# adaLN columns on VectorE alone from transposed weights, held order in the light expert steps, two output stores from ACT's queue

## The chip, the cores and the metric

The kernel runs on one core of a Trainium2 chip. The time is device microseconds of one execution, as the median of several runs. Engines are named as in the profile: PE (TensorE; PEld is its weight load), DVE (VectorE, V in the code), ACT (ScalarE, S), POOL (GpSimd, G), SP (SyncE, whose queue issues nearly all loads).

## The reference, cut to what matters

```
x: (1, 256, 1024); two layers
cond = silu(c)
for l in range(2):
    ada = cond @ w_ada[l] + b_ada[l]              # w_ada[l]: 1024 x 6144
    sh1, sc1, gt1, sh2, sc2, gt2 = split(ada, 6)
    h = rmsnorm(x, g_mix[l]) * (1 + sc1) + sh1
    z = h @ w_in[l]                               # q, k, v, forget, S5 input, two gates
    y_att = forgetting_attention(q, k, v, log_f) @ w_proj_att[l]
    y_ssm = s5(u, ...) @ w_proj_ssm[l]
    x = x + gt1 * ((g_att * y_att + g_ssm * y_ssm) @ w_out[l])
    h2 = rmsnorm(x, g_ffn[l]) * (1 + sc2) + sh2
    f = swiglu(h2, w1, w3, w2) if l == 0 else moe(h2)   # moe: top 2 of 8 experts
    x = x + gt2 * f
out = rmsnorm(x, g_final)
```

All is float32. D_FF is 2816, which the kernel cuts into 11 blocks of 256. The part in question is `ada`: 6144 columns for each layer, in 12 chunks of 512. The first four chunks of layer 0 are made at the very start by another function (`ada_first`); 20 chunks are left.

## The kernel before, in words

All 256 tokens are held on chip with the channels on partitions (`x_t`, 8 slices of 128). The weights are streamed from HBM in 1 MB loads, issued by SP in program order (`load_raw`, L211), before the MoE into a ring of three buffers `raw` (`RB = 3`). A load whose buffer is still read waits, and with it all loads behind it on SP's queue. For a product, `load_parts` splits each weight into a rounded part `wh` (ACT, L227) and a rest `wl` (DVE, L228, two instructions of 128x1024 for each load), with four buffers each, and PE takes three products for one (`dense_T`, L248).

The program has five stretches: layer 0's mixer (0 to 320 us), the dense FFN (to 495), layer 1's mixer (to 750), the MoE (to 1403, when its last load has landed) and the tail.

In the dense FFN, block j takes two loads of w13d (A and B here), 96 matmuls `mm` (L248), a gate on ACT and DVE (`fsg` L1000, `fgh` L268), and then one load of w2d (C here) and 48 matmuls `facc` (L988) for block j-1.

`ada_chunk(l, ch, E)` computes 512 adaLN columns. The tables `AT0`, `AT1` (keys are places in the mixers of layers 0 and 1) and `ATF` (block of the FFN, layer, chunk, engine) say when. With E = V it makes two loads of 1 MB through the `raw` ring, and one multiply (L324) and seven multiply-adds (L326) of 128x512 on DVE: the input channels lie on partitions, and a column of `cond` is the scalar. With E = G it makes four loads of 512 KB from POOL's queue into buffers of its own (L333), and multiplies and adds on POOL (L334, L338, L340). Either way the sum over the 128 partitions is left to `finish`, which the next chunk or `ada_flush` runs: four PE transposes (L347), four accumulating reads on ACT (L350) and an add of the bias on DVE (L351). 13 chunks are on V and 7 on G. POOL also builds the S5 tables, for layer 0 at the start and for layer 1 in the first FFN blocks.

In the MoE six lightly loaded experts run one after the other (`light`; n is 32 or 64 rows), and two heavy ones are put between their steps (`straight`). A step j of a light expert is `stage1(j)` (16 matmuls `s`, L1539, then the gate `sgS` on ACT L1544 and DVE L1545), in whose middle stands `turn_g` for block j-1 (transposes `gT`, L1527, copied to `gS` by ACT), and then `stage2(j-1)` (matmuls `y`, L1554). So stands the code; a scheduler orders the instructions of an engine, and `queued(E)` pins what is inside it behind the last instruction that engine E has been given so far. The loads go through a ring of 14 buffers of 1 MB.

`finish(ch)` (L1195 on) ends the program: the last norm, and four stores of 256 KB, all issued by SP (L1223).

Of the kernel before, what the change touches and what calls it, by code (L numbers as in the profile page):

```python
# [9 lines left out]
F32 = mybir.dt.float32  # L10
# [4 lines left out]
AF = mybir.ActivationFunctionType  # L15
# [12 lines left out]
FIRST_W = (1, 5)  # L28


AT0 = [('g1', 4, 'V'), ('g3', 5, 'V'), ('qk1', 8, 'V'), ('g2', 9, 'G'), ('p0', 6, 'V'), ('g0', 7, 'V'),
       ('o1', 10, 'V')]
AT1 = [('g0', 4, 'G'), ('g2', 5, 'V'), ('p1', 8, 'G'), ('g3', 9, 'G'), ('p0', 7, 'V'), ('o1', 10, 'V'),
       ('qk1', 11, 'G')]
ATF = [(8, 1, 6, 'G'), (6, 0, 11, 'V'), (4, 1, 2, 'G'), (7, 1, 3, 'V'), (9, 1, 0, 'V'), (1, 1, 1, 'V')]
P = 128
D = 1024
KC = 8
# [59 lines left out]


@with_exitstack  # L100
def trunk_kernel(ctx: ExitStack, tc: tile.TileContext, xT, sm, co, w_ada0, w_ada, w_in, w_v, s5bc, w_glu,
                 w_pa, w_ps, w_out, w13d, w2d, w13m, w2m, out, dbg=None, stop=None):
    nc = tc.nc
    V, S, G, PE = nc.vector, nc.scalar, nc.gpsimd, nc.tensor
# [23 lines left out]
    @contextmanager  # L128
    def queued(*engines):

        with ExitStack() as st:
            for E in engines:
                last = next((i for i in reversed(nc.cur_bb.bb.instructions) if i.engine == E.engine), None)
                if last is not None:
                    st.enter_context(tc.issue_after(last))
            yield
# [27 lines left out]
        return bank(("ms0", "ms0", "ms1", "ms1") if pair is None else (f"ms{pair}",), name)  # L164


    RB, AB, HB = 3, 2, 4
    QMAX = 2 * 520

    slots = {"raw": [(wp, "raw", RB)], "wh": [(wp, "wh", HB)], "wl": [(wp, "wl", HB)]}  # L170
# [32 lines left out]
    def load_raw(src, rows, cols):  # L203

        if ring:
            t = turn[0]
            turn[0] += 1
            return ring[t % len(ring)].rearrange("p (r c) -> p r c", r=rows)
        raw = wtile("raw", 2 * QMAX, F32)
        v = raw[:, :rows * cols].rearrange("p (r c) -> p r c", r=rows)  # L210
        nc.sync.dma_start(v, src)  # L211
        return v
# [55 lines left out]
        V.tensor_tensor(l, src, h.bitcast(F32), op=ALU.subtract)  # L268


    cond = cp.tile([P, KC], F32, name="cond")
    S.activation(cond, smv('c'), AF.Silu)
    ada = cp.tile([P, L, 48], F32, name="ada")

# [34 lines left out]
            norm_1(k, a, ada_v(0, 0), r)  # L309
        return w  # L310

    pending = []

    def ada_chunk(l, ch, E):

        ada_flush()
        if E is V:
            acc0 = lp.tile([P, 512], F32, name=nm("acc"), tag="adaacc")
            for r0 in range(0, KC, 4):
                raw = load_raw(w_ada[l * 12 + ch - 4, :, r0:r0 + 4, :], 4, 512)  # L320
                for k in range(4):
                    c = cond[:, r0 + k:r0 + k + 1]
                    if r0 + k == 0:
                        V.tensor_scalar(acc0, raw[:, k, :], c, None, op0=ALU.mult)  # L324
                    else:
                        V.scalar_tensor_tensor(acc0, raw[:, k, :], c, acc0, op0=ALU.mult, op1=ALU.add)  # L326
        else:
          with queued(G):
            acc = None
            for r0 in range(0, KC, 2):  # L330
                raw = mp.tile([P, QMAX], F32, name=nm("araw"), tag="adaraw", bufs=AB)
                raw = raw[:, :1024].rearrange("p (k c) -> p k c", k=2)
                G.dma_start(raw, w_ada[l * 12 + ch - 4, :, r0:r0 + 2, :])  # L333
                G.tensor_tensor(raw, raw, cond[:, r0:r0 + 2].unsqueeze(2).broadcast_to([P, 2, 512]), op=ALU.mult)  # L334
                if acc is None:
                    acc = raw
                else:
                    G.tensor_tensor(acc, acc, raw, op=ALU.add)  # L338
            acc0 = lp.tile([P, 512], F32, name=nm("acc"), tag="adaacc")
            G.tensor_tensor(acc0, acc[:, 0, :], acc[:, 1, :], op=ALU.add)  # L340

        def finish():
            ps = mm_ps("adaps")
            o = ada[:, l, ch * 4:ch * 4 + 4]
            b = smv('b_ada')[:, l * 48 + ch * 4:l * 48 + ch * 4 + 4]
            for j in range(4):
                PE.transpose(ps[:, j * P:(j + 1) * P], acc0[:, j * P:(j + 1) * P], ident)  # L347
            t = cp.tile([P, 4], F32, name=nm("adat"), tag="adat", bufs=2)
            for j in range(4):
                S.activation(ps[:, j * P:(j + 1) * P], ps[:, j * P:(j + 1) * P], AF.Copy, accum_out=t[:, j:j + 1])  # L350
            V.tensor_tensor(o, t, b, op=ALU.add)  # L351
        pending.append(finish)

    def ada_flush():
        while pending:
            pending.pop(0)()

    def ada_v(l, i):
        return ada[:, l, i * 8:i * 8 + 8]
# [795 lines left out]
    def moe():  # L1155
# [46 lines left out]
        def finish(ch):  # L1202

            i = fin["n"]
            fin["n"] += 1
            if i == 0:
                fin["ss"], fin["xp"] = sq_new(), [fin["a"]("xp") for _ in range(4)]
            sq_sum(fin["ss"], ch)
            xg = mo.tile([P, T], F32, name=nm("xg"), tag="pt", bufs=2)
            g = smv('g')[:, 32 + ch:33 + ch]  # L1210
            S.activation(xg, x_t[:, ch, :], AF.Copy, scale=g)
            for tb in range(2):
                PE.transpose(fin["xp"][2 * tb + ch // 4][:, (ch % 4) * P:(ch % 4) * P + P], xg[:, tb * P:(tb + 1) * P],
                             ident)
            if i < KC - 1:
                return
            y = rstd_cols(fin["ss"], ms_ps if fin["a"] is mm_ps else mm_ps)
            for tb in range(2):
                o = wtile("wh", QMAX, F32)[:, 0:1024].rearrange("p (q c) -> p q c", q=2)
                S.activation(o[:, 0, :], fin["xp"][2 * tb], AF.Copy, scale=y[:, tb:tb + 1])  # L1220
                V.tensor_scalar(o[:, 1, :], fin["xp"][2 * tb + 1], y[:, tb:tb + 1], None, op0=ALU.mult)
                for q in range(2):
                    nc.sync.dma_start(out[tb * P:(tb + 1) * P, 512 * q:512 * q + 512], o[:, q, :])  # L1223

        def small(e, n):

# [262 lines left out]
        def light(e, n, last, rk):  # L1489
# [368 lines left out]
        with c0.Else():  # L1858
# [17 lines left out]
    def tables0(i):  # L1876
        for f, j in zip(steps, TABLES_AT):
            if i == j:
                f()
    w0 = ada_first(r0)  # L1880
    with queued(V):
        tables0(0)
    for l in range(L):
        at = ADA_AT[l]
        if l:
            y = rstd_cols(sums[0])
            y = spread(y)
# [4 lines left out]
        mixer(l, (lambda i: None) if l else tables0, lambda key: ada_chunk(l, *at[key]) if key in at else ada_flush(), None if l else w0)  # L1892
        dump(f"x1_{l}", x_t)
        if l == 0:
            norm(gain_of(2, ada_v(0, 4)), ada_v(0, 3), spread(rstd_cols(sums[0])))
            ex = {j: (lambda a: lambda: ada_chunk(*a))(a) for j, a in ADA_FFN.items()}
            ex[10] = ada_flush

            def tables1():
                tabs[1] = s5_tables(1, G, G, mm_ps, ("qa", "ka", 'cum', "t8a"))  # L1900
# [23 lines left out]
            dump("x2_0", x_t)  # L1924
        if stop == l:
            return
    ada_flush()
    moe()


def pack(inp):
# [81 lines left out]
    def blocks2(w2):  # L2013
# [13 lines left out]


# [16 lines left out]
```

## Time and profile before

| | |
|---|---|
| median of three runs | 1439.9 us (1437.99 to 1440.7) |
| profiled execution, its own time | 1444.01 us |
| its span, first to last instruction | 1442.2 us |
| mean granted TensorE clock | 0.952 |
| busy: PE, DVE, ACT, POOL | 90%, 61%, 41%, 22% |
| chain that ended last: PE, DVE, ACT, issue, DMA | 70%, 17%, 5%, 4%, 2% |
| moved by DMA | 419.86 MB, mean 291 GB/s |

The busy shares are means over stretches that have different limits, so the windows view, which gives each stretch by itself, says more. The chain that ended last is read from the end backwards: each piece is the work or transfer for which the next one waited. What stands in the chain has lengthened the program; what doesn't stood beside it.

### The profile page before, as it was taken

To read this page: it belongs to the slowest core of one execution; us is meant where nothing else is said; L and a number is where in the kernel's file an instruction comes from. 1 tells how busy PE (TensorE), PEld (TensorE's weight loads), DVE (VectorE), ACT (ScalarE), POOL (GpSimd) and SP (SyncE) were. 2 spreads that over 40 slices of the span, in tenths; PEclk is the share of its full clock that TensorE was granted. 3 is DMA by queue.
4 is the path that set the end of the run, shared out by engine and by line. 5 is a ranking of instruction groups with operands and counts; after the bars stand their busy time and mean duration, and the time that the engine had idled before them with its cause. 6 is when DMAs were issued, how large, how long until landed. Compare 5 with 4: busy or idle time off the path is not lost.

```text
span 1442.2 us, 27543 instructions
## 1 busy us (share of the span) xinstructions
PE 1291.8 (90%) x11256; PEld 1050.6 (73%) x11256; DVE 881.9 (61%) x1474; ACT 592.6 (41%) x1112; POOL 316.9 (22%) x295
## 2 busy tenths in 40 slices
PE   4788999789999877799889999999999999999986
PEld 2687899779999877789878777787876555555543
DVE  7998688988786778875855544454453433433312
ACT  3455356454445654446433443343332333323212
POOL 0559215997610162414100000000000000000000
PEclk9799999979999988999989999999999999999998
DMA  8455356446786635335799999999999999999980
GB/s 308 161 177 184 115 187 232 170 152 249 245 290 242 232 121 172 111 119 196 282 381 411 420 419 394 410 420 402 402 419 421 421 421 421 418 358 422 389 323 32
DMA packets 60326, 419.86 MB, mean 291 GB/s; under 512 B 6688, under 2 KB 6688, under 8 KB 11296
## 3 DMA queue, kind: packets, MB, share of 16 engines
q1 hardware_dynamic: 56160, 403.35, 71.5%
q0 software_dynamic: 4032, 14.68, 3.2%
q8 instruction: 90, 1.47, 0.4%
q14 instruction: 44, 0.36, 0.1%
HBM read 416.95 MB, written 1.05 MB: 290 GB/s over the span
## 4 chain that ended last, share of the span: by engine, by line
PE 70%; DVE 17%; ACT 5%; issue 4%; DMA 2%; ACTq 0%; DVEq 0%
PE mm L248 18%; PE s L1539 11%; PE y L1678 6%; PE y L1554 5%; DVE wl L228 5%; PE s L1640 5%; PE s L1653 4%; PE facc L988 4%; ACT wh L227 2%; PE s L1642 2%; DMA raw<-in_w13m_dram 2%; DVE acc L326 1%; PE sc L1587 1%; PE yps L893 1%; PE gT L1527 1%
## 5 line engine op out<-in xcount | busy, mean ns | idle before, releaser
L228 DVE TENSOR_TENSOR wl<-raw,wh 128x1024 fp32r<-128x1024 f32 (+1 forms) x290 | 391.9, 1376 | 132.4 <-ACT wh L227 116.8
L227 ACT ACTIVATE wh<-raw 128x1024 fp32r<-128x1024 f32 (+1 forms) x290 | 297.6, 1054 | 210.4 <-PE mm L248 105.4
L248 PE MATMUL mm<-hh,wh 128*128 128x256 f32 x864 | 252.7, 294 | 5.1 <-ACT hh L267 2.8
L248 PE MATMUL mm<-hh,wl 128*128 128x256 f32 x864 | 251.0, 291 | 5.6 <-DVE wl L228 5.6
L248 PE MATMUL mm<-hl,wh 128*128 128x256 f32 x864 | 251.1, 291 | 2.8 <-DVE hl L426 1.8
L1539 PE MATMUL s<-raw,xeS 128*32 128x128 f32 (+1 forms) x2944 | 183.9, 316 | 1.6 <-DVE xeS L1520 0.9
L248 PEld LDWEIGHTS mm<-hh,wh 128*128 128x128 f32 x864 | 170.8, 199 | 9.7 <-ACT hh L267 3.3
L248 PEld LDWEIGHTS mm<-hh,wl 128*128 128x128 f32 x864 | 171.0, 198 | 9.1 <-DVE wl L228 6.1
L248 PEld LDWEIGHTS mm<-hl,wh 128*128 128x128 f32 x864 | 171.4, 198 | 4.8 <-DVE hl L426 2.7
L1539 PEld LDWEIGHTS s<-raw,xeS 128*32 128x32 f32 (+1 forms) x2944 | 119.6, 121 | 53.1 <-issue 11.6
L1545 DVE TENSOR_TENSOR sgS<-sgS,s 64x128 f32<-64x128 f32 (+1 forms) x66 | 23.6, 358 | 163.2 <-ACT sgS L1544 157.1
L1640 PE MATMUL s<-big,wh 128*128 128x416 f32 x352 | 107.7, 370 | 0.0
L1554 PE MATMUL y<-raw,gS 128*32 128x256 f32 (+1 forms) x744 | 93.5, 460 | 4.3 <-ACT gS L1530 4.1
L1642 PE MATMUL s<-big,wl 128*128 128x208 f32 x352 | 90.9, 258 | 0.0
L326 DVE SCALAR_TENSOR_TENSOR acc<-raw,cond,acc 128x512 f32<-128x512 f32 x91 | 81.4, 895 | 1.6
L1544 ACT ACTIVATE sgS<-s 64x128 f32<-64x128 f32 (+1 forms) x66 | 21.3, 323 | 142.6 <-PE s L1539 132.4
L1678 PE MATMUL y<-wh,ghl 128*128 128x512 f32 (+1 forms) x264 | 75.7, 407 | 3.4 <-ACT wh L227 3.2
L334 POOL TENSOR_TENSOR araw<-araw,cond 128x1024 f32<-128x1024 f32 x28 | 58.5, 2095 | 70.1 <-DMA araw<-in_w_ada_dram 70.1
L1640 PEld LDWEIGHTS s<-big,wh 128*128 128x128 f32 x352 | 66.0, 188 | 4.3 <-issue 2.9
L1642 PEld LDWEIGHTS s<-big,wl 128*128 128x128 f32 x352 | 67.2, 191 | 0.0
L1678 PEld LDWEIGHTS y<-wh,ghl 128*128 128x128 f32 (+1 forms) x264 | 45.1, 178 | 27.9 <-ACT wh L227 9.3
L988 PE MATMUL facc<-fgh,wh 128*128 128x256 f32 x352 | 62.7, 280 | 0.0
(514 smaller groups left out, 2302.8 us busy)
## 6 DMA issues: line engine op xcount, KB each, us to landing
raw<-in_w13m_dram SPq DMA_DIRECT2D x164, 1024.0 KB, 12.9
raw<-in_w2m_dram SPq DMA_DIRECT2D x82, 1024.0 KB, 12.3
raw<-in_w_ada_dram SPq DMA_DIRECT2D x32, 1024.0 KB, 5.3
raw<-in_w_in_dram SPq DMA_DIRECT2D x28, 1024.0 KB, 5.2
raw<-in_w13d_dram SPq DMA_DIRECT2D x22, 1024.0 KB, 5.3
araw<-in_w_ada_dram POOLq DMA_DIRECT2D x28, 512.0 KB, 4.5
late<-in_w13m_dram SPq DMA_DIRECT2D x12, 1024.0 KB, 13.8
raw<-in_w2d_dram SPq DMA_DIRECT2D x11, 1024.0 KB, 5.1
```

The lines of the kernel that those rows point to most:

```text
L227: S.activation(hv, rv, AF.Copy)
L228: V.tensor_tensor(lv, rv, hv.bitcast(F32), op=ALU.subtract)
L248: PE.matmul(ps, lhsT=a[k][:, c0:c0 + P], rhs=b[:, k, :], start=k == 0 and i == 0 and o % 2 == 0, stop=k == n - 1 and i == 2 and o % 2 == 1)
L326: V.scalar_tensor_tensor(acc0, raw[:, k, :], c, acc0, op0=ALU.mult, op1=ALU.add)
L334: G.tensor_tensor(raw, raw, cond[:, r0:r0 + 2].unsqueeze(2).broadcast_to([P, 2, 512]), op=ALU.mult)
L988: PE.matmul(o, lhsT=a[k][:, oc * P:(oc + 1) * P], rhs=b[:, k, :], start=j == 0 and oc % 2 == 0 and k == 0 and i == 0, stop=j == NB - 1 and ...
L1539: PE.matmul(ps[gr[g], 0:c_], lhsT=st["xe"][:, k // cb, k % cb, :], rhs=w[k][:, c_ * g:c_ * g + c_], start=k == 0, stop=k == KC - 1, tile_p ...
L1554: PE.matmul(st["y"][gr[h], 0:w_], lhsT=st["g"][:, k, :], rhs=w[k][:, w_ * h:w_ * h + w_], start=j == 0 and k == 0, stop=j == NB - 1 and k ...
L1640: PE.matmul(ps[:, 0:2 * n], lhsT=hs[k][:, o], rhs=x.rearrange("p i s -> p (i s)"), start=k == 0, stop=False)
L1642: PE.matmul(ps[:, n:2 * n], lhsT=ls[k][:, o], rhs=x[:, 0, :], start=False, stop=k == KC - 1)
L1653: PE.matmul(ps, lhsT=st["xe"][:, x_, k, :], rhs=w_[k], start=k == 0 and i == 0, stop=k == KC - 1 and i == 2)
L1678: PE.matmul(st["y"][b][h][0:s1 - s0, :], lhsT=g_[:, k, s0:s1], rhs=w[w_][k][:, h * 512:h * 512 + 512], start=j == 0 and k == 0 and i == 0, ...
```

## The change

- `w_ada` is laid out transposed: 128 output columns on the partitions and all 1024 input channels along them. `cond`, broadcast over the partitions, is a new input `cb` (512 KB, loaded once by SP after `ada_first`'s loads; ACT applies Silu to it once). A chunk is two loads of 1 MB through the `raw` ring and four DVE multiplies of 128x1024 with a sum along the row (`accum_out`), and one add of the bias. The transposes, ACT's reads, `pending`, `ada_flush` and POOL's form of the chunk are gone.
- The tables: layer 0's mixer has 6 chunks (7 before, one of them on POOL), the FFN 11, one in each block (6 before, two of them on POOL), layer 1's mixer 3 (7 before, four of them on POOL). The place `o1` has none now.
- In the light steps `turn_g`'s transposes and `stage2`'s matmuls are held with `queued(PE)` behind what PE has been given by then.
- The stores of the second 128 tokens are issued from ACT's queue.

```diff
-AT0 = [('g1', 4, 'V'), ('g3', 5, 'V'), ('qk1', 8, 'V'), ('g2', 9, 'G'), ('p0', 6, 'V'), ('g0', 7, 'V'),
-       ('o1', 10, 'V')]
-AT1 = [('g0', 4, 'G'), ('g2', 5, 'V'), ('p1', 8, 'G'), ('g3', 9, 'G'), ('p0', 7, 'V'), ('o1', 10, 'V'),
-       ('qk1', 11, 'G')]
-ATF = [(8, 1, 6, 'G'), (6, 0, 11, 'V'), (4, 1, 2, 'G'), (7, 1, 3, 'V'), (9, 1, 0, 'V'), (1, 1, 1, 'V')]
+AT0 = {'g1': 4, 'g3': 5, 'qk1': 8, 'g2': 9, 'p0': 6, 'g0': 7}
+AT1 = {'qk1': 9, 'g2': 10, 'p1': 11}
+ATF = {0: (0, 10), 1: (1, 1), 2: (0, 11), 3: (1, 0), 4: (1, 2), 5: (1, 3), 6: (1, 4), 7: (1, 5), 8: (1, 6), 9: (1, 7),
+       10: (1, 8)}
...
-    def ada_chunk(l, ch, E):
-
-        ada_flush()
-        if E is V:
-            acc0 = lp.tile([P, 512], F32, name=nm("acc"), tag="adaacc")
-            for r0 in range(0, KC, 4):
-                raw = load_raw(w_ada[l * 12 + ch - 4, :, r0:r0 + 4, :], 4, 512)
...
+    def ada_chunk(l, ch):
+
+        t = cp.tile([P, 4], F32, name=nm("adat"), tag="adat", bufs=2)
+        for h in range(2):
+            raw = load_raw(w_ada[l * 12 + ch - 4, :, 2 * h:2 * h + 2, :], 2, D)
+            for j in range(2):
+                V.scalar_tensor_tensor(raw[:, j, :], raw[:, j, :], 1.0, condb[0], op0=ALU.mult, op1=ALU.mult,
+                                       accum_out=t[:, 2 * h + j:2 * h + j + 1])
+        V.tensor_tensor(ada[:, l, ch * 4:ch * 4 + 4], t, smv('b_ada')[:, l * 48 + ch * 4:l * 48 + ch * 4 + 4], op=ALU.add)
...
-                    nc.sync.dma_start(out[tb * P:(tb + 1) * P, 512 * q:512 * q + 512], o[:, q, :])
+                    (nc.sync, S)[tb].dma_start(out[tb * P:(tb + 1) * P, 512 * q:512 * q + 512], o[:, q, :])
...
-                for k in range(2 * n // 64):
-                    PE.transpose(ps[:, k * 64:(k + 1) * 64], st["sg"][hi, k * P:(k + 1) * P], ident[hi, hi],
-                                 tile_position=(64, 0))
+                with queued(PE):
+                    for k in range(2 * n // 64):
+                        PE.transpose(ps[:, k * 64:(k + 1) * 64], st["sg"][hi, k * P:(k + 1) * P], ident[hi, hi],
+                                     tile_position=(64, 0))
...
-                for k in range(2):
-                    for h in range(G_):
-                        PE.matmul(st["y"][gr[h], 0:w_], lhsT=st["g"][:, k, :], rhs=w[k][:, w_ * h:w_ * h + w_],
-                                  start=j == 0 and k == 0, stop=j == NB - 1 and k == 1, tile_position=(0, n * h))
+                with queued(PE):
+                    for k in range(2):
+                        for h in range(G_):
+                            PE.matmul(st["y"][gr[h], 0:w_], lhsT=st["g"][:, k, :], rhs=w[k][:, w_ * h:w_ * h + w_],
+                                      start=j == 0 and k == 0, stop=j == NB - 1 and k == 1, tile_position=(0, n * h))
...
     w0 = ada_first(r0)
+    condb.append(mp.tile([P, D], F32, name="condb", tag="condb"))
+    nc.sync.dma_start(condb[0], cb)
+    S.activation(condb[0], condb[0], AF.Silu)
...
-    w_ada = np.moveaxis(rows(g['w_ada']).reshape(L, P, KC, 12, 512), 3, 1).reshape(L * 12, P, KC, 512)[4:]
+    w_ada = np.swapaxes(g['w_ada'], 1, 2).reshape(L * 12, 4, P, D)[4:].swapaxes(1, 2)
```

What the scheduler makes of it shows in the order of each engine's instructions. First DVE in the dense FFN, before, in a block that holds a chunk (block 6). `raw_4288` is load B, `raw_4310` and `raw_4316` are the two loads of the chunk, `raw_4426` is C; a row gives line, operation, output and inputs.

```order
L268 TENSOR_TENSOR fgh_4217<-fsg_4214,fgh_4217 128x512
L324 TENSOR_SCALAR acc_4309<-raw_4310,cond 128x512
L228 TENSOR_TENSOR wl_4291<-raw_4288,wh_4290 128x1024
L228 TENSOR_TENSOR wl_4295<-raw_4288,wh_4294 128x1024
L351 TENSOR_TENSOR ada<-adat_4303,sm_t 128x4
L326 SCALAR_TENSOR_TENSOR acc_4309<-raw_4310,cond,acc_4309 128x512 x3
L326 SCALAR_TENSOR_TENSOR acc_4309<-raw_4316,cond,acc_4309 128x512 x4
L228 TENSOR_TENSOR wl_4429<-raw_4426,wh_4428 128x1024
L228 TENSOR_TENSOR wl_4433<-raw_4426,wh_4432 128x1024
```

The same place after, also with one chunk in the block: `raw_4774` is B, `raw_4785` and `raw_4789` are the chunk's loads, `raw_4898` is C, and `raw_4956` is A of the next block.

```order
L317 SCALAR_TENSOR_TENSOR raw_4785,adat_4784<-raw_4785,condb 128x1024 x2
L227 TENSOR_TENSOR wl_4777<-raw_4774,wh_4776 128x1024
L227 TENSOR_TENSOR wl_4781<-raw_4774,wh_4780 128x1024
L317 SCALAR_TENSOR_TENSOR raw_4789,adat_4784<-raw_4789,condb 128x1024 x2
L319 TENSOR_TENSOR ada<-adat_4784,sm_t 128x4
L980 TENSOR_TENSOR ws<-sm_t,ada 128x64
L227 TENSOR_TENSOR wl_4901<-raw_4898,wh_4900 128x1024
L227 TENSOR_TENSOR wl_4905<-raw_4898,wh_4904 128x1024
L227 TENSOR_TENSOR wl_4959<-raw_4956,wh_4958 128x1024
L963 TENSOR_TENSOR fsg_4892<-fsg_4892,mm_4795 128x512
L227 TENSOR_TENSOR wl_4963<-raw_4956,wh_4962 128x1024
```

Before, one multiply of the chunk stands ahead of B's two splits; after, all the work on the chunk's first load does, and that on its second load stands between B's splits and C's. On SP the loads of a block follow each other as A, B, the chunk's two, C, before and after; with three buffers, C goes into B's, the chunk's first load into that of the C before it, and its second into A's. Before, blocks 1, 6, 7 and 9 have such loads; after, all eleven.

Second PE in the last light expert (64 rows), before. `s` is the first product of a block, `gT` the transposes of its gate, `y` the second product, `sc` the adding back of a heavy expert.

```order
L1714 MATMUL sc_13394<-gel_13296,big_13305 128x256 x4
L1539 MATMUL s_1869_13362<-raw_7651,xeS_7926 64x256 x8
L1539 MATMUL s_1869_13362<-raw_7652,xeS_7926 64x256 x8
L1527 MATMUL gT_13410<-co_t,sgS_13386 128x64 x2
L1714 MATMUL sc_13433<-gel_13296,big_13305 128x256 x2
L1554 MATMUL y_13272<-raw_7653,gS_13374 64x512 x4
L1714 MATMUL sc_13433<-gel_13296,big_13305 128x256 x2
L1539 MATMUL s_1874_13401<-raw_7654,xeS_7926 64x256 x8
```

And after:

```order
L1519 MATMUL y_12967<-raw_7356,gS_13017 64x512 x4
L1503 MATMUL s_1815_13057<-raw_7357,xeS_7621 64x256 x8
L1491 MATMUL gT_13066<-co_t,sgS_13029 128x64 x2
L1679 MATMUL sc_13089<-gel_12991,big_13000 128x256 x4
L1503 MATMUL s_1815_13057<-raw_7358,xeS_7621 64x256 x8
L1519 MATMUL y_12967<-raw_7359,gS_13069 64x512 x4
L1503 MATMUL s_1820_13096<-raw_7360,xeS_7621 64x256 x8
L1491 MATMUL gT_13105<-co_t,sgS_13081 128x64 x2
```

Before, the scheduler puts `gT` behind the whole of the `s` whose gate it turns; after, `gT` stands in the middle of the next block's `s`, and `y` behind that `s`. The experts with 32 rows, which run before 1085 us, keep their order but for one place; those with 64 rows all change so. The order of the MoE's loads on SP is the same.

## Rows read from the trace of the kernel before

**Rows 1.** Windows by stretch: length, then columns PE, PEld, DVE, ACT, POOL, PEclk, DMA.
```profile
0.00:320.00 320.00, 261.73 (x2040) 234.63 (x2041) 272.79 (x543) 152.43 (x295) 175.47 (x207) 0.90 0.52 186
320.00:495.00 175.00, 174.30 (x1494) 173.97 (x1494) 132.87 (x123) 83.30 (x134) 60.13 (x39) 1.00 0.71 249
495.00:750.00 255.00, 211.35 (x1775) 198.07 (x1777) 195.77 (x315) 127.62 (x256) 81.34 (x50) 0.90 0.56 200
...
1085.00:1250.00 165.00, 155.52 (x939) 91.01 (x937) 62.57 (x87) 52.54 (x86) 0.00 (x0) 1.00 1.01 421
1250.00:1403.00 153.00, 141.90 (x874) 80.59 (x872) 47.86 (x70) 38.09 (x68) 0.00 (x0) 0.99 0.96 384
```

**Rows 2.** Chain that ended last, layer 1, 495 to 690 us: start, us, what.
```profile
500.99 1.49 DVE it L395
...
511.47 2.58 DVE hl L426 x2
...
523.71 2.59 DVE hl L426
...
555.10 2.10 DVE fs L749
...
682.05 3.30 DVE wl L228
```

**Rows 3.** Timeline of POOL, the same stretch.
```profile
503.15 1.89 POOL L334 TENSOR_TENSOR araw<-araw,cond 128x1024 f32<-128x1024 f32 x1 [0.71 <-DMA araw<-in_w_ada_dram]
...
522.77 3.23 POOL L338 TENSOR_TENSOR araw<-araw,araw 128x1024 f32<-128x1024 f32 x1
```

**Rows 4.** Timeline of DVE, one short add with POOL between instructions.
```profile
503.02 0.16 DVE L398 TENSOR_TENSOR t<-y 128x2 f32<-128x2 f32 x1
```

**Rows 5.** Tiles hl and acc on DVE: duration ns min/median/max.
```profile
L426 DVE SCALAR_TENSOR_TENSOR hl<-nt,ada,hh x24: 474/560/2578, 22.2 to 523.7; 128x256 fp32r<-128x256 f32 x24
...
L326 DVE SCALAR_TENSOR_TENSOR acc<-raw,cond,acc x91: 732/752/2725, 91.1 to 735.1; 128x512 f32<-128x512 f32 x91
```

**Rows 6.** DVE, 0 to 320 us, by line and form: busy us, mean ns.
```profile
L326 DVE SCALAR_TENSOR_TENSOR acc<-raw,cond,acc 128x512 f32<-128x512 f32 x46 | 43.3, 941 | 0.6
```

**Rows 7.** DVE, 320 to 495 us, by line and form.
```profile
L228 DVE TENSOR_TENSOR wl<-raw,wh 128x1024 fp32r<-128x1024 f32 x60 | 93.6, 1591 | 32.8 <-ACT wh L227 32.8
```

**Rows 8.** Chain that ended last, dense FFN, 395 to 480 us.
```profile
414.68 5.65 PE facc L988 x48
...
420.77 11.16 PE mm L248 x96
431.93 5.67 PE facc L988 x48
```

**Rows 9.** Timeline of one FFN block that holds a chunk, 420 to 432 us.
```profile
420.81 0.49 DVE L324 TENSOR_SCALAR acc<-raw,cond 128x512 f32<-128x512 f32 x1 [2.11 <-PE adaps L347]
...
421.21 2.35 DVE L228 TENSOR_TENSOR wl<-raw,wh 128x1024 fp32r<-128x1024 f32 x2
...
423.56 5.47 DVE L326 SCALAR_TENSOR_TENSOR acc<-raw,cond,acc 128x512 f32<-128x512 f32 x7
...
423.59 0.33 SPq L211 DMA_DIRECT2D raw<-in_w2d_dram  x1
...
428.64 2.02 ACT L227 ACTIVATE wh<-raw 128x1024 fp32r<-128x1024 f32 x2 [5.20 <-DMA raw<-in_w2d_dram]
```

**Rows 10.** DMA issues of adaLN loads: KB each, median us to landing.
```profile
raw<-in_w_ada_dram SPq DMA_DIRECT2D x32, 1024.0 KB, 5.3
```

**Rows 11.** Chain that ended last, MoE, 1150 to 1260 us.
```profile
1239.03 10.07 DMA raw<-in_w13m_dram
```

**Rows 12.** Waits, 1250 to 1424 us: total us, times, longest.
```profile
PEld gT L1527 <- DVE sgS L1545: 15.2, 12, 1.4
...
PE gT L1527 <- DVE sgS L1545: 9.7, 11, 1.0
```

**Rows 13.** Timeline of SP at the end.
```profile
1434.71 2.99 SPq L1223 DMA_DIRECT2D out_dram<-wh  x4
```

More of the change, by code (lines that the diff above doesn't have):

```diff
@@ L100, in trunk_kernel @@
 @with_exitstack
-def trunk_kernel(ctx: ExitStack, tc: tile.TileContext, xT, sm, co, w_ada0, w_ada, w_in, w_v, s5bc, w_glu,
+def trunk_kernel(ctx: ExitStack, tc: tile.TileContext, xT, sm, co, w_ada0, w_ada, cb, w_in, w_v, s5bc, w_glu,
                  w_pa, w_ps, w_out, w13d, w2d, w13m, w2m, out, dbg=None, stop=None):
@@ L164, in ms_ps @@
         return bank(("ms0", "ms0", "ms1", "ms1") if pair is None else (f"ms{pair}",), name)
-    RB, AB, HB = 3, 2, 4
+    RB, HB = 3, 4
     QMAX = 2 * 520
@@ L268, in split @@
         V.tensor_tensor(l, src, h.bitcast(F32), op=ALU.subtract)
-    cond = cp.tile([P, KC], F32, name="cond")
+    cond, condb = cp.tile([P, KC], F32, name="cond"), []
     S.activation(cond, smv('c'), AF.Silu)
@@ L310, in ada_first @@
         return w
-    pending = []
-    def ada_chunk(l, ch, E):
-        ada_flush()
-        if E is V:
-            acc0 = lp.tile([P, 512], F32, name=nm("acc"), tag="adaacc")
-            for r0 in range(0, KC, 4):
-                raw = load_raw(w_ada[l * 12 + ch - 4, :, r0:r0 + 4, :], 4, 512)
[L321 to L352, printed above, removed]
@@ L354, in ada_flush @@
-    def ada_flush():
-        while pending:
-            pending.pop(0)()
+    def ada_chunk(l, ch):
[6 more added lines that the diff above has]
+        V.tensor_tensor(ada[:, l, ch * 4:ch * 4 + 4], t, smv('b_ada')[:, l * 48 + ch * 4:l * 48 + ch * 4 + 4], op=ALU.add)
@@ L1864, in moe @@
                 general()
-    ADA_AT = [{k: (c, eng[e]) for k, c, e in AT0}, {k: (c, eng[e]) for k, c, e in AT1}]
-    ADA_FFN = {j: (l, c, eng[e]) for j, l, c, e in ATF}
     nc.sync.dma_start(x_t, xT)
@@ L1883, in trunk_kernel @@
     for l in range(L):
-        at = ADA_AT[l]
+        at = (AT0, AT1)[l]
         if l:
@@ L1891, in trunk_kernel @@
         dump(f"hl{l}", hl.bitcast(F32))
-        mixer(l, (lambda i: None) if l else tables0, lambda key: ada_chunk(l, *at[key]) if key in at else ada_flush(), None if l else w0)
+        mixer(l, (lambda i: None) if l else tables0, lambda key: ada_chunk(l, at[key]) if key in at else None, None if l else w0)
         dump(f"x1_{l}", x_t)
@@ L1895, in trunk_kernel @@
             norm(gain_of(2, ada_v(0, 4)), ada_v(0, 3), spread(rstd_cols(sums[0])))
-            ex = {j: (lambda a: lambda: ada_chunk(*a))(a) for j, a in ADA_FFN.items()}
-            ex[10] = ada_flush
+            ex = {j: (lambda a: lambda: ada_chunk(*a))(a) for j, a in ATF.items()}
             def tables1():
@@ L1926, in trunk_kernel @@
             return
-    ada_flush()
     moe()
@@ L2017, in pack @@
     arrs = dict(
-        xT=rows(g['x'][0].T), sm=sm, co=co, w_ada0=w_ada0, w_ada=w_ada, w_in=w_in, w_v=w_v, s5bc=s5bc,
+        xT=rows(g['x'][0].T), sm=sm, co=co, w_ada0=w_ada0, w_ada=w_ada, cb=np.broadcast_to(g['c'][0][None], (P, D)), w_in=w_in, w_v=w_v, s5bc=s5bc,
         w_glu=rows(g['w_glu']), w_pa=rows(g['w_proj_att']), w_ps=rows(g['w_proj_ssm']), w_out=w_out,
@@ L2022, in pack @@
     return {k: np.ascontiguousarray(v) for k, v in arrs.items()}
-_ORDER = ['xT', 'sm', 'co', 'w_ada0', 'w_ada', 'w_in', 'w_v', 's5bc', 'w_glu', 'w_pa', 'w_ps', 'w_out', 'w13d', 'w2d', 'w13m',
+_ORDER = ['xT', 'sm', 'co', 'w_ada0', 'w_ada', 'cb', 'w_in', 'w_v', 's5bc', 'w_glu', 'w_pa', 'w_ps', 'w_out', 'w13d', 'w2d', 'w13m',
           'w2m']
```

## The prediction

> **What bounds the kernel now.** I read the windows by stretch first, then the chain that ended last inside each stretch, then the timelines of the engines that the chain names, and the waits last. The windows [rows 1] show five different limits. In the dense FFN PE is busy for 174.30 of 175 us: any gap that the change opens there is added to the time. The two mixers are not at any engine's limit (PE 261.73 of 320 and 211.35 of 255 us): there the chain steps from PE to DVE, ACT and loads, and a slower single instruction on it counts fully. In the MoE until 1250 us the DMA queues are full (421 GB/s) and the chain runs through transfers, one of which stands in it for 10.07 us [rows 11]: work saved on PE there is only handed to the next load. From 1250 us the rate falls to 384 GB/s [rows 1], and the chain is PE with its waits.
>
> In layer 1 the chain holds DVE instructions that are far too long for what they do [rows 2]: 1.49 us for an operation on a few columns at 500.99, while a like one at 503.02 took 0.16 [rows 4]; 2.58 us for two `hl` of 128x256, of which one takes 0.474 at best [rows 5]; 3.30 us for a split at 682.05, where two follow each other in 2.35 elsewhere [rows 9]. At the same moments POOL is in a long multiply or add of an adaLN chunk: 503.15 for 1.89 us, 522.77 for 3.23 us [rows 3]. Of the chain's DVE pieces between 495 and 690 us I count 21 such, and subtract from each the shortest of its own line: 12 pieces up to the one at 555.10 have together 18.4 us too much, the later 9, of which the one at 682.05 is the last, 13.8.
>
> **The change part by part.** The sum is made against the profiled execution's own 1444.0 us, which lies 4.1 us above the median of 1439.9.
>
> *Layer 1's mixer: POOL falls silent.* Its four chunks leave POOL and layer 1. The first 12 pieces are a serial chain (norm, first product, forget gates) with nothing beside it: I take back all 18.4 us. The later pieces lie where attention, the S5 scan and weight splits run side by side, so something else is soon late; I take half of 13.8. Together −25 us. Bounds: −12 (half of the first, a fifth of the second) and −34 (all). The three V chunks that stay replace three of 7 multiply-adds each; four products of 128x1024 cost as much, see below, and cancel.
>
> *What an instruction of the new form costs.* The trace has no multiply with a row sum. The nearest rows are multiply-adds of two full SBUF operands: 128x256 at best 0.474 us, 128x512 0.732 [rows 5], so 256 columns more cost 0.258 and 128x1024 would be 1.25. I take 1.38 with the reading of the sum, hence 2.75 for a pair on one load. Lower end 1.25; upper end twice that, 2.5, if the second full operand and the sum can't be streamed together.
>
> *Layer 0's mixer.* Six chunks on V instead of six on V and one on POOL. A V chunk was 0.49 [rows 9] plus seven at 0.941 [rows 6], about 7.1 us; four new ones under the same contention are 6 to 7. One chunk fewer of POOL's, no transposes in the chain (0.44 us a chunk, two of them in it), and one more load of 512 KB and one Silu of 128x1024 at the start (about 1 us by ACT's split of that size, half of 2.02 [rows 9]): −6, with −14 and +4 as ends.
>
> *Dense FFN.* Here the change adds work: 11 chunks instead of 6. PE loses the transposes: a step from one `facc` to the next took 431.93 − 414.68 = 17.25 us [rows 8], of which `facc` 5.65 and `mm` 11.16, so 0.44 were the transposes of a chunk and 16.81 is what PE needs. But with three buffers the loads of a block form a loop: the chunk's first load needs the buffer of the C before it; DVE, by its new order, does that load's pair ahead of B's splits; those free the buffer for C; C lands, is split, and frees the next chunk's buffer. Every wait is now a head of DVE's queue, behind which B's splits, then C's, stand, for which PE waits. Round the loop: load 5.3 [rows 10], pair 2.75, B's splits 2.35, C's load 5.05 (issue at 423.59 to ACT's start at 428.64), ACT's first half 1.01, C's splits 2.35 [rows 9]; sum 18.8. Before, only one multiply of 0.49 stood ahead of B's splits [rows 9], which makes the same loop 16.5, below PE's 17.25: it did not bind, by some 0.7 us. Now it binds by 18.8 − 17.25 = 1.6 us a block; nine steps between blocks give +14.5. POOL's chunks no longer slow the splits (mean 1.591 against 1.18 in a pair of 2.35 [rows 7, 9], but POOL still builds the tables for layer 1 in the first blocks): −1. Blocks 0 and 1 get a chunk while the tables run: +2. Together +16; ends 0 (loads land sooner than the median) and +28 (the pair 0.7 us longer under POOL, and loads of 5.9).
>
> *Held order in the light steps.* Before, `gT` stood right behind the `s` whose gate it turns, so that PE waited for ACT's Silu and DVE's product; after, half of the next `s` lies between. From 1250 us on these waits are 9.7 us, 11 times, counted at the matmul (15.2 at its weight load, of which part overlaps) [rows 12]. I take −10. The order changes for the experts of 64 rows alone. Their part before 1250 us is paced by transfers and gives nothing. The end on the other side is 0: `y` now comes one half step later, and each frees its buffer of the ring later. The end at −16 is what DMA could give: 153 us × (1 − 384/421) = 13 [rows 1], plus the last steps, in which no load is awaited.
>
> *Stores.* Four issues stand on SP one behind another for 2.99 us [rows 13]. Two on ACT's queue go beside them: −1; ends −2 and 0.
>
> Sum: −25 − 6 + 16 − 10 − 1 = −26, so 1418 for an execution like the profiled one and 1414 for the median.
>
> **Rivals.**
>
> *The multiply with row sum runs at half rate.* Then it costs 2.5 us instead of 1.38. In the FFN a pair costs 2.25 more, for nine steps +20. In the mixers it is nine chunks of four, each 1.1 us longer, +40 on DVE, of which I put half on the chain: +20. The sum is −26 + 40 = +14: 1454. It becomes slower from the point where 26 us are eaten: 18 instructions in the FFN's steps and half of 36 in the mixers, so 26/36 = 0.72 us more, at 2.1 us each. For it: no row has the form, and the sum is a third thing to do for each element. [...] Chance 0.15.
>
> *The FFN's loop does not bind.* If loads land well under their median when fewer are in flight, the block falls to PE's 16.81, and the FFN is 4 us shorter rather than 16 longer, less 2 for the first blocks: −2 in place of +16, sum −44, 1396. For it: the loads' 5.3 is a median over times at which two are in flight. Against it: A and B follow on the same queue at once. Chance 0.15.
>
> *POOL's going gives half, and the MoE's tail is paced by transfers.* In layer 1 other work is late where DVE was: −12. In the MoE the loads stay 2.5 us apart (1 MB at 421 GB/s) and the waits of PE only move: −3. Sum −12 − 6 + 16 − 3 − 1 = −6, 1434. For it: the mixers' chain changes engines often, and the DMA share is 0.96 even in the late MoE [rows 1]. Chance 0.20.
>
> **How the numbers follow.** A measurement of this kernel can tell about 0.2%, 3 us, from no change. The forecast has chance 0.50, with its own range of 1402 to 1426 from the ends of its terms taken at half. The rivals have 0.15 (1454), 0.15 (1396) and 0.20 (1434). The range from 1391 to 1440 takes in the second and third rival and leaves out the first. Faster: the forecast and the two rivals below 1437, 0.85 less what of the third and of an overfull FFN ends within 3 us of the old time, so 0.80; the same 0.05; slower 0.15.
>
> **What would show it.** POOL without any row in layer 1 but its copy and memset, and the chain from 495 to 555 us shorter by about 18 us; DVE's short operations there back at 0.2 us. The new multiply at 1.25 to 1.5 us: at 2.1 or above the forecast is wrong in sign. In the FFN `facc` starts 18.5 to 19 us apart with PE waiting for DVE's splits of B and C, and those for loads; at 16.9 the second rival holds. In the last MoE stretch no wait of `gT` for the gate above 0.3 us, and the last load landing some 8 to 10 us earlier after the start of the stretch; if it lands as late as before, the tail was paced by transfers. At the end two stores on ACT's queue.

## The result, and the profile after

The changed kernel takes 1397.4 us (1393.9 to 1400.2, four runs) against 1438.95: a ratio of 0.9709, 95% interval 0.9683 to 0.9734, 41.5 us less. The prediction said 1414 in a range of 1391 to 1440; the result lies in it, but below the forecast's own 1402 to 1426. The profiled execution of the changed kernel took 1396.7 us (span 1394.5), 47.3 below that of before, which lay about 5 above its own median. All ratios here leave out two disturbed executions, one of before (1452 us, beside e1 to e4) and one of e10 (2332 us). By stretches, with the landmarks of the trace (first `facc`; first `x_t` of the FFN's fold; first `s` of the MoE; end):

| stretch | before | after | change | predicted |
|---|---|---|---|---|
| layer 0's mixer | 328.4 | 322.2 | −6.2 | −6 |
| dense FFN | 162.8 | 163.6 | +0.8 | +16 |
| layer 1's mixer | 261.9 | 236.5 | −25.4 | −25 |
| MoE and tail | 689.1 | 672.3 | −16.8 | −11 |

The windows of after answer to [rows 1], with the bounds moved to where its stretches begin:

```profile
0.00:322.00 322.00, 270.67 (x2083) 242.17 (x2084) 263.90 (x558) 148.89 (x246) 156.40 (x189) 0.93 0.54 194
322.00:489.00 167.00, 164.83 (x1393) 164.63 (x1392) 134.09 (x167) 69.88 (x81) 27.69 (x21) 0.99 0.82 296
489.00:722.00 233.00, 210.12 (x1756) 197.49 (x1754) 153.37 (x317) 119.11 (x203) 1.17 (x2) 0.90 0.52 190
1052.00:1217.00 165.00, 157.69 (x951) 92.58 (x948) 65.45 (x90) 55.66 (x88) 0.00 (x0) 1.00 1.01 421
1217.00:1372.00 155.00, 149.57 (x968) 84.95 (x966) 46.03 (x71) 37.31 (x70) 0.00 (x0) 1.00 0.92 380
```

In layer 1 (third row) POOL's column has gone from 81.34 to 1.17 us and DVE's from 195.77 to 153.37. In the FFN (second) the loads rose from 249 to 296 GB/s and PE is still busy nearly all the time (164.83 of 167 us). The last row ends after the last MoE load, which now lands 638.1 us after the first `s` instead of 649.7.

The chain of layer 1 that answers to [rows 2], and then groups of DVE in that layer (busy us, mean ns), `hl` before and two after:

```profile
495.47 0.18 DVE it L358
...
496.20 0.17 DVE t L361
...
500.96 13.82 PE mm L247 x96
```
```profile
L426 DVE SCALAR_TENSOR_TENSOR hl<-nt,ada,hh 128x256 fp32r<-128x256 f32 x8 | 8.5, 1090 | 0.6 <-ACT hh L425 0.6
```
```profile
L389 DVE SCALAR_TENSOR_TENSOR hl<-nt,ada,hh 128x256 fp32r<-128x256 f32 x8 | 3.6, 481 | 0.6 <-ACT hh L388 0.6
...
L361 DVE TENSOR_TENSOR t<-y 128x2 f32<-128x2 f32 x3 | 0.5, 161 | 0.1
```

The operation that took 1.49 us takes 0.18. The first product starts at 500.96, 15.2 us after the fold's first `x_t`; before it was 20.3. The end of the prediction's first 12 pieces (`fs`, L749 before) now comes 51.2 us after that `x_t` instead of 66.0: 14.8 us sooner, where 18.4 was taken. The new multiply, in the FFN, by line and form:

```profile
L317 DVE SCALAR_TENSOR_TENSOR raw<-raw,condb 128x1024 f32<-128x1024 f32 x36 | 44.7, 1279 | 13.6 <-DMA raw<-in_w_ada_dram 13.6
L317 DVE DVE_READ_ACCUMULATOR raw<-raw,condb 128x1 f32 x36 | 3.0, 82 | 0.0
```

It costs 1.28 us on average and the separate reading of the sum 0.08 more, where 1.38 was taken for both. One FFN block, first SP, then DVE, to be held against [rows 9]:

```profile
375.91 3.60 SPq L210 DMA_DIRECT2D raw<-in_w_ada_dram  x2
383.57 0.33 SPq L210 DMA_DIRECT2D raw<-in_w2d_dram  x1
385.84 2.62 SPq L210 DMA_DIRECT2D raw<-in_w13d_dram  x2
391.91 4.52 SPq L210 DMA_DIRECT2D raw<-in_w_ada_dram  x2
```
```profile
381.16 1.23 DVE L317 SCALAR_TENSOR_TENSOR raw<-raw,condb 128x1024 f32<-128x1024 f32 x1 [1.40 <-DMA raw<-in_w_ada_dram]
...
382.31 1.22 DVE L317 SCALAR_TENSOR_TENSOR raw<-raw,condb 128x1024 f32<-128x1024 f32 x1
...
383.45 2.36 DVE L227 TENSOR_TENSOR wl<-raw,wh 128x1024 fp32r<-128x1024 f32 x2
...
389.52 2.36 DVE L227 TENSOR_TENSOR wl<-raw,wh 128x1024 fp32r<-128x1024 f32 x2 [1.02 <-ACT wh L226]
```

Read the two together. C's load (w2d) is issued at 383.57, when the chunk's first pair has ended and B's splits have only begun (383.45, to 385.81): C goes into the buffer of the chunk's first load. The next w13d load, A of the next block, goes out at 385.84, the end of B's splits. Before, C's load went out at 423.59, the end of B's splits [rows 9]. What was said of the three buffers ahead of the prediction (C into B's) holds before and not after: the pool gives a load the buffer that its order lets go first, and the order of DVE had changed. The chain shows `facc` 16.9 us apart, as against 17.25 in [rows 8]; of the nine steps in this profile eight take 16.8 to 16.9, and one, in block 1, 20.9:

```profile
444.45 5.65 PE facc L951 x48
461.37 5.67 PE facc L951 x48
```

In the late MoE, a step of the last expert in the chain, and the only wait of `gT` for the gate that is left from 1217 to 1374 us, where [rows 12] had 15.2 and 9.7 us:

```profile
1357.16 0.27 PE gT L1491 x2
1357.43 1.88 PE s L1503 x16
1359.31 1.72 PE y L1519 x8
1361.02 1.73 PE s L1503 x16
1362.75 0.26 PE gT L1491 x2
```
```profile
PEld gT L1491 <- DVE sgS L1509: 0.8, 1, 0.8
```

PE goes from one instruction to the next, 5.6 us a step. The stores, as in [rows 13]:

```profile
1386.94 2.25 SPq L1186 DMA_DIRECT2D out_dram<-wh  x2
```

Two more come from ACT's queue at 1387.52. The last lands 6.0 us after the first issue; before it was 5.6.

### The profile page after: what moved, and what is told of

Same layout as the page of the kernel before. It is cut to its first block, busy times and chain, and to the rows that moved or that the text cites. A ratio compares the mean times of both kernels' runs of the same rounds, so it can differ in the third digit from the quotient of the medians.

```text
span 1394.5 us, 27210 instructions
## 1 busy us (share of the span) xinstructions
PE 1282.1 (92%) x11176; PEld 1045.1 (75%) x11176; DVE 830.6 (60%) x1530; ACT 567.0 (41%) x955; POOL 185.3 (13%) x211
## 4 chain that ended last, share of the span: by engine, by line
PE 75%; DVE 13%; ACT 5%; DMA 3%; issue 2%; ACTq 0%; DVEq 0%
PE mm L247 20%; PE s L1503 12%; PE y L1643 6%; PE y L1519 5%; DVE wl L227 5%; PE s L1605 5%; PE s L1618 4%; PE facc L951 4%; ACT wh L226 3%; PE s L1607 2%; DVE raw L317 2%; PE mm L696 2%; PE yps L856 1%; DMA raw<-in_w13m_dram 1%; PE mm L260 1%
## 5 line engine op out<-in xcount | busy, mean ns | idle before, releaser
L227 DVE TENSOR_TENSOR wl<-raw,wh 128x1024 fp32r<-128x1024 f32 (+1 forms) x290 | 358.9, 1261 | 123.3 <-ACT wh L226 100.9
L317 DVE SCALAR_TENSOR_TENSOR raw<-raw,condb 128x1024 f32<-128x1024 f32 x80 | 101.8, 1295 | 15.9 <-DMA raw<-in_w_ada_dram 15.9
L1494 ACT ACTIVATE gS<-gT 128x64 f32<-128x64 f32 (+1 forms) x66 | 16.4, 248 | 126.3 <-PE gT L1491 126.0
L1519 PEld LDWEIGHTS y<-raw,gS 128*32 128x32 f32 (+1 forms) x744 | 31.9, 120 | 36.9 <-issue 20.1
## 6 DMA issues: line engine op xcount, KB each, us to landing
raw<-in_w13m_dram SPq DMA_DIRECT2D x164, 1024.0 KB, 13.8
```

The lines of the kernel that those rows point to most:

```text
L227: V.tensor_tensor(lv, rv, hv.bitcast(F32), op=ALU.subtract)
L317: V.scalar_tensor_tensor(raw[:, j, :], raw[:, j, :], 1.0, condb[0], op0=ALU.mult, op1=ALU.mult, accum_out=t[:, 2 * h + j:2 * h + j + 1])
```

## The experiments

The trace left open why the FFN's loop did not bind, whether layer 1's gain was POOL's, and what the hold is worth. The same code gives times that lie some us apart from one set of executions to the next (the changed kernel 1397.4 and, in e9, 1390.6), so stretches and ratios are compared. A stretch is read from one profile of each kernel; where other profiles run the same code in a stretch, their spread is given.

**e1, the changed kernel with the FFN's order by hand.** C's loads are emitted right behind `dense_T`, the chunk takes B's splits as a function between its halves, and the splits of B and the multiplies are each held with `queued(V)`.

```diff
+            cut(0)
+            if j in extra:
+                extra[j](lambda: cut(1))
...
+            early = load_w(w2[prev[0]], 2, 1024, 1) if prev else None
```

> The changed kernel with its order in the dense FFN written out by hand: A's splits, the chunk's first pair, B's splits, the chunk's second pair, C's splits on VectorE; the raw buffers are given out as in the changed kernel, C's load into the buffer of the chunk's first load. Both theories: nothing changes, 1397 us give or take 3, FFN steps of 16.84 to 16.95 us. It is the control for the two kernels run beside it.

1396.4 us, FFN 164.5 us: a fair control. Its chain shows how near the edge the loop is: where a chunk's load takes 7.6 us, it is in the chain.

```profile
428.82 7.61 DMA raw<-in_w_ada_dram
```

**e2, e1 with a longer loop.**

```diff
+                    if between and not h:
+                        V.tensor_tensor(raw[:, j, :], raw[:, j, :], raw[:, j, :], op=ALU.max)
```

> As e1, with one more VectorE instruction of 128x1024 ahead of each multiply on a chunk's first load (two a block, 2.4 us). Theory (loop): the steps are set by the round chunk load 5.2, its pair 2.4, C's load 4.8, ACT 1.1, C's splits 2.4, which is 16.0 in the changed kernel and just hidden under PE's 16.84; 2.4 more makes it 18.4, so about nine steps of 18.4 instead of 16.9, FFN 13 to 15 us longer, 1410 to 1412. Rival (no loop, only VectorE's busy time counts): VectorE has 16.84 minus about 13.5 free in a block, the 2.4 fit in, under 3 us in all, 1397 to 1400.

FFN 185.1 us, 20.6 more than e1; 1420.5 us, 24 more, which is above the loop's 1410 to 1412 and far from the rival's 1397 to 1400. SP's issues of one round:

```profile
401.55 4.80 SPq L210 DMA_DIRECT2D raw<-in_w_ada_dram  x2
412.54 0.33 SPq L210 DMA_DIRECT2D raw<-in_w2d_dram  x1
...
420.85 4.95 SPq L210 DMA_DIRECT2D raw<-in_w_ada_dram  x2
```

A round takes 19.3 us, 0.9 more than expected, since the chunk's load lands after 6.0 and not 5.2 us. The loop is real; DVE's free time does not absorb the extra work.

**e3, e1 with the buffers strictly in turn.**

```diff
-        raw = wtile("raw", 2 * QMAX, F32)
...
+        raw = rawb[seen["raw"] % RB]
+        seen["raw"] += 1
```

> As e1, but the three raw buffers are used strictly in turn, so that C's load waits for B's splits, which stand behind the chunk's first pair: the loop that the prediction reckoned with. Theory (the prediction's loop was right for that turn, and wrong only in who gets which buffer): steps of 18.6 to 19.5, FFN 15 to 22 us longer, 1412 to 1420. Rival (the loads land earlier than reckoned, or something else hides the round): steps stay below 17.5, 1397 to 1403.

1434.1 us, FFN 197.8 us, 33 more than e1, steps of 20.5 to 21.6 us but for the first and the last; ratio to before 0.9964 (0.9946 to 0.9983). The chain of one round:

```profile
399.73 5.43 DMA raw<-in_w_ada_dram
...
406.41 1.23 DVE raw L325 x3
...
409.94 7.84 DMA raw<-in_w2d_dram
...
417.87 1.06 ACT wh L231
...
418.98 6.10 PE facc L959 x35
```

These are the pieces that the prediction added up, in its order: chunk load, its pair, B's splits, C's load, ACT. C's load takes 7.8 us instead of 5.05, so the round is longer still than 18.8. Here the order of the loads has changed too: in the fixed turn the next block's A takes the buffer of the chunk's first load and is issued ahead of C (407.67), and its B 2.3 us behind C. That these two lengthen C's load is likely, but no run parts them from the turn. With the turn and the order of loads that comes with it the change would have lost nearly all that it gains.

**e4 and e12, the hold alone and the hold undone.** e4 adds to the kernel before, and e12 takes from the changed one:

```diff
+                with queued(PE):
+                    for k in range(2 * n // 64):
+                        PE.transpose(...)
...
+                with queued(PE):
+                    for k in range(2):
```

> The kernel before with the held order in the light steps alone. Theory (PE's waits for the gate let the loads run dry in the late MoE, and no wait is left after): the whole late gain of the changed kernel comes with it, the last load 10 to 12 us earlier after the first s, the tail 4 to 5 us shorter, in all 14 to 17 us, 1422 to 1425. Rival (only the 9.7 us of waits counted at the matmul come back, the rest of the late gain is from loads that start earlier for want of adaLN loads ahead of them): 8 to 11 us, 1428 to 1431.

> The changed kernel with the hold in the light steps undone. Theory (waits of PE plus the loads that run dry behind them: 12 us up to the last load and 5 behind it): the MoE from its first s to the end is 687 to 690 us instead of 672, 14 to 17 us longer in all. Rival (the prediction's 10: the waits counted at the matmul, and nothing else): 681 to 683 us, 9 to 11 us longer.

e4: 1428.3 us, ratio 0.9936 (0.9907 to 0.9966), MoE 677.3 us against 689.1. e12: 1405.8 us, ratio 0.9786 (0.9744 to 0.9828) against 0.9709 and 0.9665 (e9) with the hold, MoE 686.0 against 672.3 to 676.7 in three profiles with it. The waits are back to the digit of [rows 12]:

```profile
PE gT L1490 <- DVE sgS L1508: 9.7, 11, 1.0
```

By the whole MoE both give about 12 us, between what the two theories said. The traces part it better. But for one place, the order differs only behind the last product `s` of the first heavy expert (L1640 before), which starts about 290 us after the first `s` of the MoE. From there to the end it takes 398.8 us (before) and 396.8 (e12) without the hold, and 382.7 to 386.1 in the eleven profiles with it: 11 to 16 us. Up to the landing of the last load it is 359.3 and 357.1 against 349.3 to 352.0, and behind that 39.5 and 39.7 against 32.5 to 35.3.

**e5 and e6, POOL's arithmetic taken out and put back.** The order on all other engines is that of their base.

```diff
+                if l and ch in (4, 8, 9, 11):
+                    acc = raw
+                    continue
                 G.tensor_tensor(raw, raw, cond[:, r0:r0 + 2].unsqueeze(2).broadcast_to([P, 2, 512]), op=ALU.mult)
```
```diff
...
+            for i in range(4):
+                for k in range(4):
+                    G.tensor_tensor(a, a, cond[:, 2 * k:2 * k + 2].unsqueeze(2).broadcast_to([P, 2, 512]), op=ALU.mult)
+                    if k:
+                        G.tensor_tensor(a, a, a, op=ALU.add)
```

> The kernel before, without POOL's multiplies and adds of the four adaLN chunks in layer 1's mixer (their loads, one small add each and all else stay; these 2048 columns of adaLN are wrong). The order on every other engine is the same. Theory (POOL's long instructions stretch VectorE's on the chain): layer 1, from the first x_t of the FFN's fold to the first s of the MoE, falls from 261.9 us to 232 to 244; the run is 18 to 30 us faster, 1409 to 1421. Rival (layer 1 gained from fewer and moved chunks, transposes and loads): within 4 us of the kernel before.

> The changed kernel, with the arithmetic of four chunks put back on POOL in layer 1 (16 multiplies and 12 adds of 128x1024 on a buffer of its own, no loads, no result used), starting when the FFN's fold is done; the order on every other engine is the same. Theory (POOL against VectorE): 28 instructions of 2.0 to 2.7 us fill 495 to 560 us, the 12 serial pieces are long again, layer 1 is 18 to 25 us longer than 236.5, 1415 to 1422 in all. Rival (the gain was not POOL's): under 4 us.

In e5 other tokens reach other experts, so the MoE runs another path and its 1597 us say nothing; layer 1 is measured to the end of its last product. It falls from 248.9 to 210.0 us, 39 less: more than the 25 of the change. By the landmark `fs` 14.2 of these come in the first part and 24.7 behind it. In e6 the same stretch rises from 224.7 to 250.2 and the run to 1418.9 us, ratio 0.9888 (0.9856 to 0.9919). The rival of both is out. DVE in e6, 490 to 555 us, while POOL runs with no gap above 0.1 us until 550.8, and then the like rows of the changed kernel, 490 to 540 us:

```profile
L401 DVE SCALAR_TENSOR_TENSOR hl<-nt,ada,hh 128x256 fp32r<-128x256 f32 x8 | 14.3, 1813 | 0.6 <-ACT hh L400 0.6
...
L694 DVE COPY U<-uT 32x256 f32<-32x256 f32 x4 | 8.0, 1989 | 0.1
...
L399 DVE SCALAR_TENSOR_TENSOR nt<-x_t,a,rstd 128x256 f32<-128x256 f32 x8 | 3.5, 472 | 0.8 <-PE rstd L384 0.8
...
L673 DVE COPY m<-kps 32x128 f32<-32x128 f32 x4 | 1.2, 290 | 0.1
```
```profile
L389 DVE SCALAR_TENSOR_TENSOR hl<-nt,ada,hh 128x256 fp32r<-128x256 f32 x8 | 3.6, 481 | 0.6 <-ACT hh L388 0.6
L387 DVE SCALAR_TENSOR_TENSOR nt<-x_t,a,rstd 128x256 f32<-128x256 f32 x8 | 3.6, 476 | 0.8 <-PE rstd L372 0.7
...
L682 DVE COPY U<-uT 32x256 f32<-32x256 f32 x4 | 1.5, 381 | 0.1
...
L661 DVE COPY m<-kps 32x128 f32<-32x128 f32 x4 | 1.2, 290 | 0.2
```

`hl` and `U`, whose operands all lie in SBUF, take 3.8 and 5.2 times as long. `nt` and `m`, each with an operand in PSUM, take what they took.

**e7, no chunk in FFN block 1.**

```diff
-AT1 = {'qk1': 9, 'g2': 10, 'p1': 11}
+AT1 = {'g0': 8, 'qk1': 9, 'g2': 10, 'p1': 11}
...
```

> The changed kernel with no adaLN chunk in FFN block 1 (the later ones move up, and chunk 8 of layer 1 goes to place g0 of layer 1's mixer). In the changed kernel block 1 took 20.9 us against 16.85, while POOL still built tables. Theory (the chunk's work under POOL's contention sets that block): 4 us back in the FFN, and 2 to 3 lost in layer 1, 1394 to 1397. Rival (the contention alone sets it, the chunk is hidden): nothing in the FFN, 2 to 3 us lost, 1399 to 1401.

1398.35 us, ratio 0.9735 (0.9712 to 0.9758), between the two forecasts; FFN 165.3, layer 1 3 us longer. Nothing came back in the FFN, as the rival said. Its block 1 takes 19.2 us without a chunk; with one, seven profiles that share the changed kernel's FFN give 16.9 to 22.7. So what the chunk costs there stays open.

**e8, all stores on SP.**

```diff
-                    (nc.sync, S)[tb].dma_start(out[tb * P:(tb + 1) * P, 512 * q:512 * q + 512], o[:, q, :])
+                    nc.sync.dma_start(out[tb * P:(tb + 1) * P, 512 * q:512 * q + 512], o[:, q, :])
```

> The changed kernel with all four stores on SP's queue again. Prediction's term: the stores are worth 1 us, so from the first store's issue to the end 8.5 us instead of 7.6. Rival (the first store issued is not the last to land by the issue alone, the stores are worth nothing): 7.4 to 7.7 us, as in the kernel before.

One execution: from the first store's issue to the end 9.7 us, to the last landing 5.9, against 7.6 and 6.0 in the changed kernel and 7.5 and 5.6 before. The landing does not move; the rest is time behind it, 3.8, 1.6 and 1.9 us. Ten profiles with two stores on ACT's queue have 6.4 to 7.6 us to the end, and e4 and e5, with all on SP, 7.6 and 6.2. The two groups overlap, so a gain of the stores is not shown.

**e9 to e11, the places of layer 1's chunks.** e5 left a question: with POOL silent and the chunks of before on DVE, layer 1 took 210.0 us, in the changed kernel 224.7. Its chain holds:

```profile
531.29 6.94 DMA raw<-in_w_ada_dram
540.80 1.14 DVE raw L317 x2
544.49 1.14 DVE raw L317 x2
660.34 2.29 DVE raw L317 x4
667.32 7.88 DMA raw<-in_w_out_dram
```

A chunk's load and multiplies at qk1, multiplies at p1, and behind them w_out's load. e9 is the changed kernel again.

```diff
-AT1 = {'qk1': 9, 'g2': 10, 'p1': 11}
+AT1 = {'g2': 9, 'p0': 10, 'o1': 11}
```
```diff
+AT1 = {'g2': 9, 'g3': 10, 'p0': 11}
```

> The changed kernel itself, as the control for the two run beside it: 1394 to 1400 us, layer 1 from the first x_t to the end of its last product 219 to 225 us.

> The changed kernel, its three chunks of layer 1 at the places that VectorE's chunks had before: g2, p0, o1 instead of qk1, g2, p1. Theory (with POOL silent, what is left in layer 1 above the 210 us of e5 is the places: a chunk load of 6.9 us and two pairs at qk1, and at p1 a pair and w_out's load of 7.9 us behind the chunk's): 8 to 12 us back in layer 1, some 2 of it lost to o1's loads between the first of the MoE: 1385 to 1391. Rival (the new multiply and its whole-megabyte loads cost that wherever they stand): within 3 us of the control.

> As e10, with the places g2, g3, p0. Theory: 6 to 12 us back in layer 1, nothing between the first loads of the MoE, 1385 to 1391. Rival: within 3 us of the control.

e9: 1390.6 us, ratio 0.9665 (0.9629 to 0.9701), layer 1 to its last product 221.6. e10: 211.7, the 10 us that the theory said, but the MoE takes 680.7 us instead of 674.4, where 2 us more were expected. So the total does not change, as its rival had it; the ratio is 0.9668 (0.9642 to 0.9694). This stands at the head of its MoE in the chain:

```profile
711.34 15.85 DMA raw<-in_w13m_dram
```

e11: 210.8, MoE 674.0, **1380.1 us**, ratio 0.9597 (0.9575 to 0.9619): 10 us faster than the changed kernel beside it, and the best version here. No chunk load and no multiply is left in its layer 1 chain among the long pieces.

## Why the prediction was right, and where not

The direction and the largest term held, but the total was forecast 17 us too high for the median and 21 for the profiled execution, and one right number was so by errors that cancel.

*POOL in layer 1: mechanism shown, size by luck.* e5 and e6 show that POOL's long instructions stretch DVE's. The term of −25 was measured at −25.4. But the silence alone is worth 39 us (e5). The first 12 pieces gave 14.2 of the 18.4 that were taken back in full (14.8 in the changed kernel); behind them it gave 24.7, where half of 13.8 was taken, so much came from instructions that the count of 21 left out. Against that stood the item put at nothing ("replace ... and cancel"): at their new places the three chunks cost 10 to 11 us more than at those of e10 and e11. In the chain of the changed kernel the two loads shown (a chunk's, and w_out's behind another) have 14.8 us and the multiplies 4.6, so the loads on SP's queue are the likelier part; no run moves one without the other. A multiply's price says nothing of the load that it waits for and that waits ahead of the next one.

*Dense FFN: the step that failed* is "those free the buffer for C". C took the buffer of the chunk's first load instead. The round is then chunk load 5.2, pair 2.4, C's load 4.75, ACT 1.1, C's splits 2.4: 16.0 us from 375.91 to 391.91, under PE's 16.84. The prediction's own sum without B's splits is 16.45. So +16 became +0.8. e3 forces the turn that the prediction assumed and gives 20.5 to 21.6 a step: with it the forecast of +16 would have been too small. The second rival (the loop does not bind, 1396) came true in its number, and not for its reason, for the loads took about what was said.

The loop is hidden only just. The round shown is the shortest in this trace; others take up to 18.1 us, made up for by shorter ones. In e9, the same kernel again, the steps are 16.8 to 18.7 us and the FFN takes 166.1. The first half of its chain goes round the loop: a chunk's load of 7.34 us at 387.67, for one, and then C's of 4.87 at 397.44. There the chunk's first load landed after 6.2 to 7.3 us six times in a row.

*Held order: right mechanism, a size off.* −10 was taken; in the stretch where it acts the hold gives 11 to 16 us (e4, e12, and the profiles beside them). What PE's waits cost is not their sum alone, since a buffer freed late also sends the next load late (in the kernel before, from 1250 us on, SP's loads wait 35.7 us for `s` and 31.8 for `y`): more than half of the gain shows in when the last load lands (359.3 and 357.1 against 349.3 to 352.0 us). Of the 16.8 us by which the MoE got shorter, 14.9 lie in that stretch and 1.9 ahead of it. Up to there profiles of the changed kernel's MoE take 288.3 to 290.6 us (e10 apart), and before and e4, which share that code, 290.3 and 293.5. e10 takes 297.6: the new chunk at o1 costs some 8 us there. The load of 15.85 us that e10 has in its chain is not in that of before, so that o1's old chunk cost before anything like it is not shown.

*Layer 0:* −6.2 against −6, but the ten profiles with the changed layer 0 spread from 314.1 to 323.7 (mean 318.2), and the three with that of before from 324.3 to 328.4 (mean 327.0). So −9 is nearer, and none of its parts was tried alone.

*The multiply at half rate* is out. It takes 1.22 us where POOL is silent (mean of 12 in layer 1 of the changed kernel), about what a split takes that has two full SBUF operands and no sum (2.36 for two). The rival's 2.5 us and the 0.13 that the forecast's 1.38 held for reading the sum were the author's estimates: the longest of the changed kernel's 80 multiplies took 2.06 (median 1.22), and the reading 0.08.

*Stores:* −1 was taken, and nothing shown.

## What to carry to other kernels

Who gets a buffer is part of the order: before adding up a loop of loads, find from issue times, or from the built program, which instruction frees the buffer that each load takes, and do so again after a change of order. An engine that is off the chain can still set it (POOL's arithmetic alone made layer 1 25.5 us longer in e6): look for instructions on the chain that are longer than the shortest of their own line, and at what else runs just then. When work moves to another engine or layout, its loads move too; try its places one by one, for here they were worth 10 us with the same instructions (e9 against e11).

## What the runs showed of the hardware

That POOL slows DVE was in the trace of before (`hl` took 474 to 2578 ns [rows 5]); that it slows only some of DVE's instructions the prediction did not say. In e6, under POOL's multiplies and adds, `hl`, with two different SBUF operands, took 3.8 times as long (481 to 1813 ns) and the copy `U` from SBUF to SBUF 5.2 times (381 to 1989), while `nt` and `m`, each with an operand in PSUM, did not change (476 and 472, 290 and 290). `hl` and `nt` are both SCALAR_TENSOR_TENSOR of 128x256, and `U` and `m` are both copies, so where the operands lie is the likely difference; no run shows what it rests on. Beside that, a sum along the row cost one more instruction of 0.08 us (82 ns at L317).
